# A hybrid attention, SSD and RG-LRU block on one core: first loads in two pieces, matmuls on zeros ahead of them, one more projection chunk ahead of the step sizes, and projection banks that stay open into the chunked scan

## The chip, the core and the metric

The kernel runs on one NeuronCore of a Trainium2 chip. The metric is the device time of one execution in microseconds (us), as the median of several runs. The engines are named as the profile names them: PE (TensorE's matmuls), PEld (its weight loads), DVE (VectorE), ACT (ScalarE), POOL (GpSimd) and SP (the queue that starts the DMAs).

## What is computed

One layer on 1024 tokens of width 1024. The input is normalised and multiplied with `w_in`; the columns of the product go to dilated attention, to a state space mixer (SSD) with its step sizes `dt`, and to a gated recurrence (LRU). The three results go through `w_out`, then a gated feed-forward layer and a last norm follow.

```python
h = rmsnorm(x, norm_mix)
q, k, v, z, xbc, dt_raw, g_lru, x_lru = split_cols(h @ w_in)
att = dilated_attention(q, k, v)
ssd = ssd_mixer(z, xbc, dt_raw, ssd_conv_w, ssd_conv_b, ssd_dt_bias, ssd_a_log, ssd_d, ssd_norm)
lru = rglru_mixer(g_lru, x_lru, lru_conv_w, lru_conv_b, lru_wa, lru_ba, lru_wx, lru_bx, lru_lambda)
x = x + concatenate([att, ssd, lru]) @ w_out
x = x + swiglu(rmsnorm(x, norm_ffn), w_gate, w_up, w_down)
return rmsnorm(x, norm_final)

# in ssd_mixer: a convolution and silu over xbc, the step sizes, and a scan in chunks of 128 tokens
xbc = silu(causal_depthwise_conv(xbc, conv_w, conv_b))
dt = softplus(dt_raw + dt_bias)
acs = cumsum(dt * a, axis=2)          # inside each chunk
```

## The kernel before

**Tiling.** Everything lies with channels on the 128 partitions and the 1024 tokens along a row. A float32 operand is held as a high and a low part (`hi`, `lo`, written by `split` and `wload`: the high part is an ACT copy, the low part a DVE subtraction), and each product is three matmuls: high by high, high by low, low by high. One projection chunk is 128 output columns of `w_in`: two halves of 512 tokens, each 8 x 3 matmuls of 128 x 512, 48 in all. Each half has a PSUM bank of its own, taken in turn from three (`bank`, the pool `psl`, tile name `mm`), and DVE empties it with a multiply by the norm (`e<-mm,rB`).

**First stage (lines 180 to 241).** For each of the 8 row blocks of x, `xt` is loaded, DVE or ACT writes the high part of `h` (`hi`), DVE the low part, ACT the squares. As they come, `early` puts the products of two chunks (28 and 24) into banks, and those of a third (29) afterwards. The load of x's block 0 and that of the first weights are one DMA of 512 KB each.

**The LRU and SSD chunks (lines 287 to 404).** Four LRU chunks follow; each ends in the two gate products of line 333, whose banks (pool `ps2`, two tiles `p2`) ACT reads with a sigmoid (`ri<-p`). The eight chunks that the SSD needs are called by `xbc`: `in_proj`, then `conv` (an ACT pass and three DVE passes, in the profile `bct<-e,pr` or `xs<-e,pr` at lines 78 and 268), then a silu on ACT, which needs its function table loaded. Two of the eight (`NXB = 2`) are called beside the last LRU chunk; six (`for c in XB`) after the step sizes.

**The step sizes (lines 353 to 397).** A bank pair `pd` from `ps2` takes 32 small matmuls (lines 360 to 364). ACT copies 8 rows of it (`e<-p 8x1024`), DVE adds 8 others and multiplies with the norm (`e<-p,e 8x1024` and `e<-e,rB 8x1024`), and PE transposes the result (line 370). Softplus on DVE and two more small products (lines 382, 386, 394) lead to `acs`. A DMA writes it out (`acd`), and DMAs read it back to all partitions (`acb`).

**The chunked scan (lines 407 to 577).** `pctx.close()` ends the pools of the projections. A new pool of three banks (`psm`, line 446) and the scan's own pools are opened. The scan's small steps are interleaved with units of `qkv_fill` (line 409), large products for attention (matmuls of line 423). The first unit needs the high and low parts of two weight tiles, w_in[8] and w_in[9].

**What sets the order.** The code is in program order; a scheduler then places the instructions of each engine in one fixed list, from their dependencies and its own estimates of time. Each engine takes its list in order, so an instruction that waits holds back all behind it.

Of the kernel before, what the change touches and what calls it, by code (L numbers as in the profile page):

```python
# [7 lines left out]
F32 = mybir.dt.float32  # L8
# [30 lines left out]
def tile_hybrid_block(ctx: ExitStack, tc: tile.TileContext, xT, w_in, w_dt, w_out, w_gu, w_dn, lru_g, prm,  # L39
# [8 lines left out]
    wp = ctx.enter_context(tc.tile_pool(name="wp", bufs=2))  # L48
    sm = ctx.enter_context(tc.tile_pool(name="sm", bufs=2))
    dr = ctx.enter_context(tc.tile_pool(name="dr", bufs=1, space=DRAM))  # L50
    pctx = ExitStack()
    psm = pctx.enter_context(tc.tile_pool(name="psl", bufs=3, space=PSUM))
    ps2 = pctx.enter_context(tc.tile_pool(name="ps2", bufs=2, space=PSUM))
    ps1 = pctx.enter_context(tc.tile_pool(name="ps1", bufs=1, space=PSUM))

# [9 lines left out]
    def f(ap):  # L65
        return ap.bitcast(F32)
# [10 lines left out]
    def act(out, in_, func, **kw):  # L77
        return A.activation(out=out, in_=in_, func=func, **kw)  # L78
# [5 lines left out]
    def wload(src, pool=None, le=None):  # L84
        st = wp.tile([P, S], F32, name="wst", tag="wst", bufs=2)
        dma(out=st, in_=src)
        hi = (pool or wp).tile([P, S], F32R, name="whi", tag="whi", bufs=2)
        lo = (pool or wp).tile([P, S], F32R, name="wlo", tag="wlo", bufs=2)
        split(st, hi, lo, le or V)
        return hi, lo  # L90
# [89 lines left out]
    with tc.tile_pool(name="np", bufs=2) as npool:  # L180
        sqs = []
        wdt = const.tile([P, KD, 40], F32R, name="wdt")
        V.memset(f(wdt), 0.0)
        wd = npool.tile([P, 64], F32, name="wd", tag="wd", bufs=1)
        p2t = [ps2.tile([P, S], F32, name="p2", tag="p2") for _ in range(2)]
        outs = [[t[:, :H2], t[:, H2:]] for t in p2t]
        outs.insert(1, [bank() for _ in range(2)])
        w01 = []

        def early(kk, which):  # L190
            ws = slice(kk * P, kk * P + P)
            for j in which:
                (whi, wlo), os = w01[j], outs[j]
                for n, (w, a) in enumerate(((whi, hhi[kk]), (whi, hlo[kk]), (wlo, hhi[kk]))):
                    for hf in range(2):
                        last_mm[0] = T.matmul(os[hf], lhsT=w[:, ws], rhs=a[:, hf * H2:hf * H2 + H2],  # L196
                                              start=(kk == 0 and n == 0), stop=(kk == KD - 1 and n == 2))

        last_mm = [None]
        for k in range(KD):  # L200
            xt = slot(npool, "xt", bufs=4)
            dma(out=xt, in_=xT[k * P:k * P + P, :])
            if k == 0:
                w01.append(wload(w_in[28]))
            if k == 1:
                w01.append(wload(w_in[24]))
                dma(out=ident, in_=c_ident)
                V.tensor_copy(identr, ident)
            if k == 4:
                w01.append(wload(w_in[29], pool=npool))  # L210
            hi, lo = slot(hp, "h", F32R), slot(hp, "h", F32R)
            if k % 2:
                act(hi, xt, AF.Copy, scale=pc("g_mix", k))
            else:
                V.tensor_scalar(out=hi, in0=xt, scalar1=pc("g_mix", k), scalar2=None, op0=ALU.mult)
            V.scalar_tensor_tensor(out=lo, in0=xt, scalar=pc("g_mix", k), in1=f(hi), op0=ALU.mult, op1=ALU.subtract)
            hhi.append(hi)
            hlo.append(lo)
            sqs.append(slot(npool, "sq", bufs=8))
            last_act = act(sqs[k], xt, AF.Square)  # L220
            for kk in ([0, 1] if k == 1 else range(k, k + 1) if 0 < k < KD - 1 else ()):
                early(kk, (0, 1))
        for k in range(1, KD):
            add(V, sqs[0], sqs[0], sqs[k])
        dma(out=wd, in_=w_dt)
        wdv = wd.rearrange("p (k c) -> p k c", c=8)
        act(wdt[:, :, 0:8], wdv, AF.Copy)
        sub(V, wdt[:, :, 32:40], wdv, f(wdt[:, :, 0:8]))
        rn = rnorm_small(sqs[:1], 1024.0, 1e-6, ps1)
        V.tensor_copy(rtok, rn)  # L230
        early(KD - 1, (0, 1))
        for hf in range(2):
            pb = spread(ps1.tile([P, H2], F32, name="p1", tag="p1"), rn[:, 4 * hf:4 * hf + 4])
            V.tensor_copy(rB[:, hf * H2:hf * H2 + H2], pb)
        for k in range(KD):
            early(k, (2,))
        xp0, g0, xp1 = ev(), ev(), ev()
        for dst, o in zip((xp0, g0, xp1), outs):
            for hf in range(2):
                sl = slice(hf * H2, hf * H2 + H2)  # L240
                mul(V, dst[:, sl], o[hf], rB[:, sl])
# [110 lines left out]

    dma(out=tri, in_=c_tri)
    dma(out=elast, in_=c_last)
    dtr = ev()[0:8, :]
    pd = ps2.tile([P, S], F32, name="p2", tag="p2")
    for hf in range(2):
# [85 lines left out]
            next(gen, None)  # L443

    pctx = ExitStack()
    psm = pctx.enter_context(tc.tile_pool(name="psm", bufs=3, space=PSUM))
    fill = qkv_fill()
    dsk = pc("dskip", 0, 4)
    wctx = ExitStack()
# [134 lines left out]
    next(fill)  # L584
    ssd_ctx.close()
    pctx.close()
    mm_ctx = ExitStack()
    psm = mm_ctx.enter_context(tc.tile_pool(name="psa_mm", bufs=2, space=PSUM))

# [643 lines left out]
```

## Time and profile before

| what | us |
|---|---|
| median of 3 runs (1411.64 to 1413.68) | 1412.61 |
| profiled execution, its own time | 1410.98 |
| its span, first to last instruction | 1409.2 |
| PE busy in the span | 1347.0 (96%) |
| DVE busy | 977.2 (69%) |
| ACT busy | 667.3 (47%) |
| POOL busy | 395.5 (28%) |

PE is busy for 96% of the span, so what a change can give is in the waits of PE, and in stretches where TensorE's clock is at its lower level. The profile lists who waited for whom, the instructions in order of time, the chain of work that ended last, and the granted clock of any stretch.

### The profile page before, as it was taken

Reading aid. Unit: us, or ns where it says so; the run is one execution under the profiler, and the core shown is the slowest. Engines: PE = TensorE matmul, PEld = TensorE weight load, DVE = VectorE, ACT = ScalarE, POOL = GpSimd, SP = SyncE. Lnnn points to the kernel's source line nnn. Section 1 sums busy time; section 2 is a strip of 40 time slices with the busy share of each in tenths; the row PEclk is TensorE's granted clock in tenths of the full one; section 3 lists DMA queues with packets and bytes.
Section 4 is the critical chain, followed back from the end, with each engine's and each line's share of the span. In section 5 each row is a group of like instructions: output and inputs, shape, how many; then the busy total and the mean of one; then the engine's idle time right before and its main releaser. Section 6 shows DMA issues by size and latency. Waiting matters only on the chain.

```text
span 1409.2 us, 18442 instructions
## 1 busy us (share of the span) xinstructions
PE 1347.0 (96%) x6786; PEld 1126.4 (80%) x6786; DVE 977.2 (69%) x1520; ACT 667.3 (47%) x1086; POOL 395.5 (28%) x283
## 2 busy tenths in 40 slices
PE   7999898999999999998988999999999998999996
PEld 6887688878888788887866788888877787888896
DVE  7667748988344877877696876676786765655745
ACT  5385636554233666666564433333333244543533
POOL 0022103765000000000036366665555651010103
PEclk9999999999999999999999999999999999999997
DMA  5112132342228964420364433444544357855523
GB/s 202 53 45 75 46 76 69 95 125 87 63 103 270 293 184 106 120 76 28 122 218 170 153 117 120 156 157 157 172 172 157 124 184 282 286 192 195 191 77 120
DMA packets 90266, 198.66 MB, mean 141 GB/s; under 512 B 9272, under 2 KB 23992, under 8 KB 90176
## 3 DMA queue, kind: packets, MB, share of 16 engines
q1 hardware_dynamic: 90176, 197.49, 43.1%
q8 instruction: 53, 0.87, 0.2%
q14 instruction: 37, 0.30, 0.1%
HBM read 142.64 MB, written 54.82 MB: 140 GB/s over the span
## 4 chain that ended last, share of the span: by engine, by line
PE 56%; DVE 13%; POOL 11%; DMA 8%; issue 6%; ACT 5%; SPq 0%; DVEq 0%; POOLq 0%; ACTq 0%
PE mm L98 19%; PE mm L1039 10%; PE x L911 5%; POOL t L69 5%; PE mm L911 4%; PE x L1039 3%; DMA whi<-w_gu 3%; DVE h L69 3%; PE mm L423 2%; PE pt L725 2%; PE p L196 2%; DVE wlo L69 1%; POOL t L75 1%; PE sc L681 1%; PE sc L682 1%
## 5 line engine op out<-in xcount | busy, mean ns | idle before, releaser
L98 PE MATMUL mm<-h,whi 128*128 128x512 f32 x1184 | 374.2, 395 | 1.7 <-DVE att L75 0.9
L98 PEld LDWEIGHTS mm<-h,whi 128*128 128x128 f32 x1184 | 221.2, 189 | 46.2 <-DVE e L72 1.2
L98 PE MATMUL mm<-h,wlo 128*128 128x512 f32 x592 | 232.3, 393 | 0.0
L911 PE MATMUL x<-A,h 128*128 128x512 f32 x660 | 170.0, 397 | 3.3 <-DVE h L69 2.8
L75 POOL TENSOR_TENSOR t<-whi 128x512 f32<-128x512 f32 x22 | 36.0, 1637 | 475.5 <-DMA x1d<-e 369.1
L911 PE MATMUL mm<-A,h 128*128 128x512 f32 x594 | 154.6, 400 | 2.1 <-ACT h L78 2.1
L1039 PE MATMUL mm<-h 128*128 128x512 f32 (+1 forms) x666 | 152.3, 381 | 0.0
L911 PEld LDWEIGHTS x<-A,h 128*128 128x128 f32 x660 | 123.7, 189 | 35.5 <-DVE h L69 5.2
L1039 PEld LDWEIGHTS mm<-h 128*128 128x128 f32 x666 | 122.1, 192 | 23.2
L911 PEld LDWEIGHTS mm<-A,h 128*128 128x128 f32 x594 | 112.9, 191 | 28.7 <-ACT h L78 2.5
L98 PEld LDWEIGHTS mm<-h,wlo 128*128 128x128 f32 x592 | 111.8, 189 | 23.5 <-DVE wlo L69 0.3
L911 PE MATMUL x<-h 128*128 128x512 f32 x396 | 106.5, 395 | 0.0
L69 DVE TENSOR_TENSOR h<-t,h 128x512 fp32r<-128x512 f32 x97 | 96.8, 1016 | 10.5 <-ACT h L78 10.5
L78 ACT ACTIVATE e<-x 128x512 f32<-128x512 f32 x60 | 35.7, 595 | 121.1 <-PE x L911 111.7
L69 DVE TENSOR_TENSOR h<-wst,h 128x512 fp32r<-128x512 f32 (+1 forms) x69 | 75.0, 1108 | 25.3 <-ACT h L78 23.7
L911 PEld LDWEIGHTS x<-h 128*128 128x128 f32 x396 | 75.1, 190 | 17.3
L78 ACT ACTIVATE whi<-wst 128x1024 fp32r<-128x1024 f32 x44 | 46.4, 1055 | 64.9 <-PE mm L98 52.3
L75 DVE TENSOR_TENSOR e<-mm,e 128x512 f32<-128x512 f32 x45 | 30.8, 684 | 61.3 <-POOL e L69 51.1
L69 DVE TENSOR_TENSOR wlo<-wst,whi 128x1024 fp32r<-128x1024 f32 x44 | 57.1, 1298 | 16.5 <-ACT whi L78 16.4
L69 DVE TENSOR_TENSOR h<-whi,h 128x1024 fp32r<-128x1024 f32 (+1 forms) x47 | 50.7, 1078 | 24.2 <-ACT h L78 24.1
L78 ACT ACTIVATE h<-wst 128x512 fp32r<-128x512 f32 (+1 forms) x69 | 51.9, 781 | 31.5 <-DMA whi<-sd 11.6
L1039 PE MATMUL x<-h 128*128 128x512 f32 (+1 forms) x270 | 60.8, 361 | 3.3 <-ACT h L78 3.3
(277 smaller groups left out, 2657.6 us busy)
## 6 DMA issues: line engine op xcount, KB each, us to landing
wst<-w_in SPq DMA_DIRECT2D x32, 512.0 KB, 3.7
qkl<-qkd SPq DMA_DIRECT2D x48, 256.0 KB, 5.7
wst<-w_gu SPq DMA_DIRECT2D x22, 512.0 KB, 4.3
whi<-w_gu SPq DMA_DIRECT2D x22, 512.0 KB, 5.6
wdd<-t SPq DMA_DIRECT2D x22, 512.0 KB, 4.8
sd<-wlo SPq DMA_DIRECT2D x22, 512.0 KB, 5.1
qkd<-e SPq DMA_DIRECT2D x16, 512.0 KB, 3.5
wst<-sd SPq DMA_DIRECT2D x27, 256.0 KB, 3.7
```

The costliest lines, as they stand in the source:

```text
L69: eng.tensor_tensor(out=out, in0=a, in1=b, op=ALU.subtract)
L75: return eng.tensor_tensor(out=out, in0=a, in1=b, op=ALU.add)
L78: return A.activation(out=out, in_=in_, func=func, **kw)
L98: T.matmul(ps, lhsT=w[:, ws], rhs=a[:, sl], start=(k == 0 and n == 0), stop=(k == nk - 1 and n == 2))
L196: last_mm[0] = T.matmul(os[hf], lhsT=w[:, ws], rhs=a[:, hf * H2:hf * H2 + H2], start=(kk == 0 and n == 0), stop=(kk == KD - 1 and n == 2))
L423: T.matmul(o, lhsT=a[k][:, ts], rhs=w, start=(k == 0 and n == 0), stop=(k == KD - 1 and n == 2))
L681: T.matmul(sc[:, :w], lhsT=qs[:, qc], rhs=ks[:, kc], start=True, stop=False)
L682: gate[0] = T.matmul(sc[:, :w], lhsT=qs[:, qc], rhs=kl[:, kc], start=False, stop=True)
L725: T.transpose(pt[:, j, qi * P:qi * P + P], pes[qi][:, kb * P:kb * P + P], ident)
L911: last_mm[0] = T.matmul(ps, lhsT=w[:, wi, ws], rhs=ops[k][i][:, ai], start=(start and k == 0 and n == 0), stop=(stop and k == 3 and n == 2 ...
L1039: mm = T.matmul(banks[n][:, cols], lhsT=w[:, 0, ws], rhs=a[:, 1, cols], start=(start and j == 0 and m == 0), stop=(stop and j == NP - 1 an ...
```

## The change

Four things change, and all outputs are computed as before.

1. The load of x's block 0 and that of the first weight tile are cut in two: half of x, 256 columns of weights, the other half of x, the other 768 columns. The splits of the weights, and DVE's two passes over x, follow piece by piece. Chunk 28's products of block 0 are written ahead of block 1.
2. Ten matmuls of 128 x 320 on a tile of zeros (`wdt` before it is filled) are written ahead of the first products, into a bank that the third early chunk later overwrites.
3. One more `xbc` chunk (the third of eight) is written ahead of the step sizes.
4. The pool `psl` is no longer closed ahead of the scan. The scan's `qkv_fill` keeps taking the same three banks.

```diff
-    pctx = ExitStack()
-    psm = pctx.enter_context(tc.tile_pool(name="psl", bufs=3, space=PSUM))
+    mm_ctx, pctx = ExitStack(), ExitStack()
+    psm = mm_ctx.enter_context(tc.tile_pool(name="psl", bufs=3, space=PSUM))
...
+        wu = wdt.rearrange("p k c -> p (k c)")
+        for _ in range(10):
+            T.matmul(outs[2][0][:, 0:320], lhsT=wu[:, 0:P], rhs=wu, start=True, stop=True)
...
-            dma(out=xt, in_=xT[k * P:k * P + P, :])
             if k == 0:
-                w01.append(wload(w_in[28]))
+                st = wp.tile([P, S], F32, name="wst", tag="wst", bufs=2)
+                whi, wlo = (wp.tile([P, S], F32R, name=n, tag=n, bufs=2) for n in ("whi", "wlo"))
+                w01.append((whi, wlo))
+                for sl in (slice(0, 256), slice(256, S)):
+                    ts = slice(0, H2) if sl.start == 0 else slice(H2, S)
+                    dma(out=xt[:, ts], in_=xT[0:P, ts])
+                    dma(out=st[:, sl], in_=w_in[28][:, sl])
+                    split(st[:, sl], whi[:, sl], wlo[:, sl])
+            else:
+                dma(out=xt, in_=xT[k * P:k * P + P, :])
...
-            for kk in ([0, 1] if k == 1 else range(k, k + 1) if 0 < k < KD - 1 else ()):
-                early(kk, (0, 1))
+            if k == 1:
+                early(0, (1,))
+            if k < KD - 1:
+                early(k, (0,) if k == 0 else (0, 1))
...
     dma(out=tri, in_=c_tri)
     dma(out=elast, in_=c_last)
+    xbc(XB.pop(0))
     dtr = ev()[0:8, :]
...
     pctx = ExitStack()
-    psm = pctx.enter_context(tc.tile_pool(name="psm", bufs=3, space=PSUM))
     fill = qkv_fill()
...
     pctx.close()
+    mm_ctx.close()
     mm_ctx = ExitStack()
```

The two DVE passes over x's block 0 (lines 215 and 216) run once per half in the changed code; the diff of those lines is left out here.

What this makes of the engines' lists is seen best around the step sizes. On PE, 21 of the third SSD chunk's 48 matmuls already stood ahead of the step sizes' 32; now all 48 do, and 37 of the next chunk stand between the step sizes and the transposes, as before. On ACT this stood between the end of the last LRU chunk and the step sizes (`la` is that chunk's gate, `e<-p 8x1024` the copy of the step sizes, `bct<-e,pr` the convolution of the third SSD chunk, the second `bct<-bct` its silu):

```order
L78 ACT_TABLE_LOAD
L78 ACTIVATE bct<-bct 128x1024
L78 ACT_TABLE_LOAD
L78 ACTIVATE la_1021<-la_1021 128x1024
L78 ACTIVATE e<-p_1037 8x1024
L78 ACTIVATE whi<-wst 128x1024
L78 ACTIVATE bct<-e,pr 128x1024
L78 ACTIVATE sp_1084<-dt 128x64
```

and now stands, on ACT at the same place:

```order
L78 ACT_TABLE_LOAD
L78 ACTIVATE bct<-bct 128x1024
L78 ACT_TABLE_LOAD
L78 ACTIVATE la_1037<-la_1037 128x1024
L78 ACTIVATE whi<-wst 128x1024
L78 ACTIVATE bct<-e,pr 128x1024
L78 ACT_TABLE_LOAD
L78 ACTIVATE bct<-bct 128x1024
L78 ACTIVATE e<-p_1117 8x1024
```

The copy of the step sizes has moved behind the third SSD chunk's weights, convolution, table load and silu. On DVE this stood from the last LRU chunk's scan (line 345) to the step sizes' two passes over 8 x 1024:

```order
L72 TENSOR_TENSOR ri<-la_1021,ri 128x1024
L345 SCALAR_TENSOR_TENSOR la_1021<-la,ri 128x1024
L72 TENSOR_TENSOR e<-mm,rB 128x512
L75 TENSOR_TENSOR e<-p_1037,e 8x1024
L72 TENSOR_TENSOR e<-e,rB 8x1024
```

and now stands, on DVE at the same place (the scan's line is 360 in the changed file, the convolution's 283):

```order
L72 TENSOR_TENSOR ri<-la_1037,ri 128x1024
L360 SCALAR_TENSOR_TENSOR la_1037<-la,ri 128x1024
L72 TENSOR_TENSOR e<-mm,rB 128x512
L69 TENSOR_TENSOR wlo<-wst,whi 128x1024
L283 SCALAR_TENSOR_TENSOR bct<-e,pr,bct 128x1021
L283 SCALAR_TENSOR_TENSOR bct<-e,pr,bct 128x1022
L283 SCALAR_TENSOR_TENSOR bct<-e,pr,bct 128x1023
L75 TENSOR_TENSOR e<-p_1117,e 8x1024
L72 TENSOR_TENSOR e<-e,rB 8x1024
```

The same chunk's low weights and three convolution passes have come in between. Behind the step sizes the lists of PE hold 77 projection matmuls up to the product of line 382 (87 before), and 103 from the last transposes of line 394 to the scan (122 before); from there on the lists are nearly the same.

## Rows read from the trace of the kernel before

**Rows 1.** Waits of PE up to 260 us: who waited, total us, times, longest.

```profile
PE p L196 <- ACT whi L78: 7.7, 1, 7.7
PE p L360 <- ACT ri L78: 5.6, 1, 5.6
```

**Rows 2.** Timeline of the first stage: start, length, engine, line, operation.

```profile
9.53 1.28 DVE L216 SCALAR_TENSOR_TENSOR h<-xt,pr,h 128x1024 fp32r<-128x1024 f32 x1 [0.59 <-ACT h L78]
...
10.46 1.91 PE L196 MATMUL p<-h,whi 128*128 128x512 f32 x4
...
12.17 1.05 PE L196 MATMUL p<-h,wlo 128*128 128x512 f32 x2
...
12.66 1.22 DVE L69 TENSOR_TENSOR wlo<-wst,whi 128x1024 fp32r<-128x1024 f32 x1
...
14.67 0.63 PE L196 MATMUL mm<-h,wlo 128*128 128x512 f32 x2
```

**Rows 3.** The chain that ended last, 130 to 235 us: start, length, what.

```profile
145.05 0.65 PE p L360
...
154.94 8.41 PE mm L98 x37
163.35 0.59 PE p L370 x8
...
189.06 0.89 PE p L394 x8
...
193.40 13.32 DMA acb<-acd
```

**Rows 4.** Busy times by stretch; before the last two numbers the granted clock and DMA.

```profile
143.30:150.10 6.80, 5.05 (x12) 1.85 (x13) 3.16 (x3) 6.73 (x7) 2.68 (x1) 0.50 0.26 80
...
221.80:225.20 3.40, 2.90 (x13) 2.93 (x14) 3.40 (x12) 3.38 (x5) 1.27 (x2) 0.50 0.00 0
```

**Rows 5.** Timeline of PE ahead of the step sizes and at the scan.

```profile
139.03 0.39 PE L98 MATMUL mm<-h,wlo 128*128 128x512 f32 x1
...
222.30 0.76 PE L423 MATMUL mm<-whi,h 128*128 128x256 f32 x2 [3.00 <-DVE e L72]
```

**Rows 6.** Timeline of ACT around the step sizes.

```profile
138.14 1.28 ACT L78 ACT_TABLE_LOAD   x1 [5.61 <-DVE bct L268]
139.44 1.06 ACT L78 ACTIVATE bct<-bct 128x1024 f32<-128x1024 f32 x1
...
154.28 1.06 ACT L78 ACTIVATE la<-la 128x1024 f32<-128x1024 f32 x1
155.37 1.02 ACT L78 ACTIVATE e<-p 8x1024 f32<-8x1024 f32 x1
```

**Rows 7.** Timeline of DVE around the step sizes and at the scan.

```profile
131.17 3.06 DVE L69 TENSOR_TENSOR wlo<-wst,whi 128x1024 fp32r<-128x1024 f32 x1
134.16 3.90 DVE L268 SCALAR_TENSOR_TENSOR bct<-e,pr,bct 128x1021 f32<-128x1021 f32 x3
...
156.71 2.29 DVE L345 TENSOR_TENSOR_SCAN la<-la,ri 128x1024 f32<-128x1024 f32 x1
158.91 0.67 DVE L72 TENSOR_TENSOR e<-mm,rB 128x512 f32<-128x512 f32 x1
159.50 1.20 DVE L75 TENSOR_TENSOR e<-p,e 8x1024 f32<-8x1024 f32 x1
160.73 1.87 DVE L72 TENSOR_TENSOR e<-e,rB 8x1024 f32<-8x1024 f32 x1
...
163.13 1.20 DVE L69 TENSOR_TENSOR wlo<-wst,whi 128x1024 fp32r<-128x1024 f32 x1
...
224.74 1.21 DVE L69 TENSOR_TENSOR wlo<-wst,whi 128x1024 fp32r<-128x1024 f32 x1
```

**Rows 8.** Timeline of POOL: its multiplies in the last two LRU chunks.

```profile
130.75 2.40 POOL L72 TENSOR_TENSOR g<-la,g 128x1024 f32<-128x1024 f32 x1 [9.17 <-DVE la L345]
...
159.13 2.40 POOL L72 TENSOR_TENSOR g<-la,g 128x1024 f32<-128x1024 f32 x1 [10.37 <-issue]
```

More of the change, by code (lines that the diff above doesn't have):

```diff
@@ L211, in tile_hybrid_block @@
             hi, lo = slot(hp, "h", F32R), slot(hp, "h", F32R)
[L212 to L216, printed above, removed]
+            for ts in ((slice(0, H2), slice(H2, S)) if k == 0 else (slice(0, S),)):
+                if k % 2:
+                    act(hi, xt, AF.Copy, scale=pc("g_mix", k))
+                else:
+                    V.tensor_scalar(out=hi[:, ts], in0=xt[:, ts], scalar1=pc("g_mix", k), scalar2=None, op0=ALU.mult)
+                V.scalar_tensor_tensor(out=lo[:, ts], in0=xt[:, ts], scalar=pc("g_mix", k), in1=f(hi[:, ts]),
+                                       op0=ALU.mult, op1=ALU.subtract)
             hhi.append(hi)
```

## The prediction

> **What bounds the kernel now.** I read the busy shares first: PE is busy for 96% of the span, so the waits of PE are what can be won. Up to the scan they are few. PE starts at 7.7 us, when the first weights have been split, and waits 5.6 us ahead of the step sizes for a gate's bank [rows 1]; the scan's first unit waits 3.00 us for DVE to empty a bank [rows 5]. Next I read the pace. The first matmuls of 128 x 512 come (12.17 - 10.46) / 4 = 0.43 us apart [rows 2], later ones 8.41 / 37 = 0.227 [rows 3], so TensorE begins at the lower of its two levels (1.2 instead of 2.4 GHz). It falls back to it after the two waits: the granted clock is 0.50 in 143.3 to 150.1 us and in 221.8 to 225.2 [rows 4]. All three places are aimed at. Last I read the chain that ended last. From the step sizes to the scan it does not stay on PE: it leaves the last transposes, passes the DMA `acb` of 13.3 us and returns to PE at the scan [rows 3]. So ACT, DVE and a DMA are near the bound there too, and what PE wins it keeps only where they keep pace.
>
> **Start.** The first pieces of x and of the weights let PE begin some 2.5 us sooner. But block 1 of x is not loaded earlier: the bytes ahead of it are the same. Its low part ends on DVE at 9.53 + 1.28 = 10.81 [rows 2]. Chunk 28's 6 matmuls of block 0 are then done; of block 1's 6 matmuls, 4 follow that low part, so at the lower level they end near 10.81 + 4 x 0.43 = 12.5, where before they ended at 12.17 + 2 x 0.43 = 13.0: 0.5 us won. At the full level they would end sooner, but PE then needs the low weights of chunk 24, which DVE ends at 12.66 + 1.22 = 13.88; before, those matmuls began at 14.67 [rows 2]. So at most 0.8 us is won however early PE starts. Two more DMAs ahead of block 1 and three more DVE instructions can cost some 0.3. I take a gain of 0.4 (0.8 to a loss of 0.3). The ten matmuls on zeros lie where PE was idle, cost nothing, and can only move the clock.
>
> The Trainium skill ("TensorE: Matmul & The Clock Gate", Part 1, on what is actually happening) says that the throttled clock is the default and that activity releases it; by that the zeros make the first 12 matmuls run at full pace, 12 x 0.2 = 2.4 us, and the sum below would be 2.0 lower. The rows of the feed speak against it.
>
> **The chunk ahead of the step sizes: PE.** The last projection matmul before the wait starts at 139.03 [rows 5], so PE is free at 139.26. The 27 matmuls that are moved in fill 27 x 0.227 = 6.13 us, to 145.39. The bank is free at 145.05 [rows 3]: the wait is gone. The 32 small matmuls now run at full pace, about 32 x 0.23 = 7.36, to 152.75, and the 37 behind them take 8.41, to 161.16. There the transposes of line 370 could start; before, they started about 163.3 [rows 3].
>
> **The chunk ahead of the step sizes: ACT and DVE.** The transposes need the step sizes, and the order of ACT and DVE has put the third SSD chunk ahead of them, as the lists in the section on the change show. From the rows of before: DVE's scan of the last LRU chunk ends at 156.71 + 2.29 = 159.0, the emptying of a bank at 159.6 [rows 7]. Then come the low weights. POOL multiplies from 159.13 to 161.53 [rows 8]. When the same DVE instruction met POOL's multiply of 130.75 to 133.15, it took 3.06 us and ended 1.08 after it, against 1.20 alone [rows 7, 8]; so it ends near 162.6. The convolution takes 3.90 [rows 7], to 166.5. ACT's table load waits for it (the row of 138.14 does the same, 0.08 us after a convolution's end), 1.28 long, and the silu takes 1.06 behind it [rows 6], to 168.95; the copy of the step sizes takes 1.02, to 170.0, where before it ended at 156.4 [rows 6]. DVE adds (1.20, to 171.2) and multiplies. That row is 1.87 long, but POOL was at work then and is not now, so I take 1.2 [rows 7, 8]: 172.4. PE would wait from 161.2 to 172.4, 11.2 us, twice what was removed.
>
> Compared by progress: the transposes start 172.4 - 163.3 = 9.1 us later, with 6.13 us more of PE's work done before them: 3.0 lost. The lower bound has low weights that POOL does not hold (1.9 less): 1.1 lost. The upper has the multiply at 1.87: 3.7 lost. All instructions of this chain hang on the last LRU chunks' gates and so on PE; they move with the gain at the start.
>
> **The clock after that wait.** The 163.3 of before already holds the slow restart of the step sizes: 12 matmuls at 0.43 instead of 0.23, 2.4 us. A wait of 11 us brings the lower level at least as surely, and the projection matmuls behind the transposes pay it: again 2.4, at least 1.4 (half of the 2.9 busy us in the second stretch of rows 4), at most 3.4 (half of a 6.8 us stretch). So this edit costs 3.0 + 2.4 = 5.4 us (1.1 + 1.4 = 2.5 to 3.7 + 3.4 = 7.1).
>
> The Trainium skill ("ScalarE: Activation LUTs", What ACT_TABLE_LOAD costs) counts a drain of about 1.38 us to each load. The row does not show it: load at 138.14, 1.28 long, next instruction at 139.44 [rows 6]. With it the sum would be 1.4 higher.
>
> **The banks kept into the scan.** If the wait of 3.00 and the slow restart after it (1.4) went, 4.4 would be won. What is late next: the unit needs the second weight's low part, and DVE ends that at 224.74 + 1.21 = 225.95 [rows 7], 36.0 us after the last transposes (189.06 + 0.89 = 189.95 [rows 3]). In the changed lists one convolution no longer stands behind `acb`, so that DVE work comes about 3.9 us sooner after the transposes, at 32.1. PE has 122 - 103 = 19 matmuls fewer in between, 4.3 us. The two nearly cancel: PE starts the unit early, does 12 matmuls, then waits for DVE. I take nothing, from a gain of 1.0 to a loss of 1.2. The chunk order costs no DMA: SP's list past the start is the same.
>
> **The sum.** -0.4 + 5.4 + 0 = +5.0 us. The profiled execution of 1410.98 would become 1416.0. The median of the runs stands 1.6 above it, and I add the 5.0 to the median: 1412.6 + 5.0 = **1417.6 us**. Its bounds: 2.5 - 0.8 - 1.0 = +0.7 (1413.3) to 7.1 + 0.3 + 1.2 = +8.6 (1421.2). Past the scan the lists are nearly the same and PE's waits there hang on chains that shift as a whole, so nothing gives the loss back.
>
> **Rivals.**
>
> *The waits simply go* (faster). The start wins 0.8, the step sizes 5.6 + 2.4, the scan 4.4: 13.2 us, 1399.4. It speaks for it that the profile names these waits singly. It decides at the transposes: the step sizes would have to be ready by 161.2, and the rows give 172.4. A shift of 11 us in lists that each engine takes in order is not to be seen. 6%; another 3% lie between this and the next.
>
> *Near enough to nothing* (same). The chain at its lower bound, +2.5, and the kept banks worth about half of their 4.4, with the start at -0.4: about 0, 1412.6. It decides at the scan: DVE would have to bring the second low weights some 2 us sooner than the 32.1 above. For it: the wait's row names only the bank. 19%.
>
> *The wait moves on once more* (slower). The product of line 382 waits for softplus on DVE. That chain starts 9.1 us later, and PE has 77 instead of 87 matmuls (2.3 us less) ahead of it. With the slow restart PE just stays behind it by my count; if DVE needs 3 us more, mixed with two more convolutions, PE waits there too: 1420.6. 12%.
>
> **How the numbers follow.** The forecast, with its bounds, has 60%, the rivals 6 + 3, 19 and 12. About 0.2% (2.8 us) is what a measurement of this kernel tells from no change. Faster by more: 6 and 2 of the 3, 0.08. Within: 19, the third of the 3, and 3 from the forecast's low end, 0.23. Slower by more: 57 + 12, 0.69. The range leaves out the first rival and the farthest ends: 1411.5 to 1421.0.
>
> **What would show it.** In the changed profile the wait of line 360's successor is gone, and PE waits some 11 us ahead of the transposes of 8 x 1024 (line 386 there), with a granted clock of 0.5 behind it; ACT's copy `e<-p 8x1024` follows the silu of `bct` and a table load. The scan's first unit starts without a wait and stops after 12 matmuls for DVE. PE meets chunk 24's low weights at most 0.8 us sooner than at 14.67. I am wrong if PE passes the transposes with a wait under 6 us, or if the first stage wins over 1 us.

## The result: 0.8% slower, 11.4 us

Measured side by side on one chip, the kernel before took 1413.14 us (median of 4 runs, 1411.64 to 1414.73) and the changed kernel 1424.81 (4 runs, 1423.98 to 1426.88). The ratio is 1.0081, with a 95% interval of 1.0068 to 1.0094: 11.4 us lost (9.6 to 13.3). The direction and the main place were forecast, the size was not: 5.0 us were forecast, 8.4 at most.

The profiled execution of the changed kernel took 1426.88 us. Of its page, the span and the busy times (engine, us, share, instructions):

```profile
span 1425.1 us, 18469 instructions
PE 1357.5 (95%) x6796; PEld 1135.5 (80%) x6796; DVE 979.6 (69%) x1523; ACT 666.5 (47%) x1086; POOL 392.6 (28%) x283
```

PE is busy 10.5 us longer (1347.0 before). The ten small matmuls on zeros are 3.0 of them; the rest is the same list of matmuls done at a lower clock. Next, the waits of PE up to 260 us in the changed kernel (who waited for whom, total us, times, longest), against [rows 1]:

```profile
PE p L386 <- DVE e L72: 11.4, 1, 11.4
PE mm L439 <- DVE e L72: 2.2, 1, 2.2
PE p L199 <- ACT h L78: 1.9, 1, 1.9
...
PE mm L439 <- DVE wlo L69: 1.3, 1, 1.3
PE p L199 <- DVE h L227: 0.7, 1, 0.7
```

The wait of 5.6 us ahead of the step sizes is gone, and one of 11.4 stands ahead of the transposes of line 386. The timeline of ACT, DVE and PE there (start, length, engine, line, operation, in brackets the wait just before it):

```profile
157.37 1.04 ACT L78 ACTIVATE whi<-wst 128x1024 fp32r<-128x1024 f32 x1
161.62 3.11 DVE L69 TENSOR_TENSOR wlo<-wst,whi 128x1024 fp32r<-128x1024 f32 x1
164.65 3.91 DVE L283 SCALAR_TENSOR_TENSOR bct<-e,pr,bct 128x1021 f32<-128x1021 f32 x3
168.64 1.28 ACT L78 ACT_TABLE_LOAD   x1 [5.66 <-DVE bct L283]
169.93 1.06 ACT L78 ACTIVATE bct<-bct 128x1024 f32<-128x1024 f32 x1
171.01 1.01 ACT L78 ACTIVATE e<-p 8x1024 f32<-8x1024 f32 x1
172.06 1.21 DVE L75 TENSOR_TENSOR e<-p,e 8x1024 f32<-8x1024 f32 x1 [3.50 <-ACT e L78]
173.31 1.21 DVE L72 TENSOR_TENSOR e<-e,rB 8x1024 f32<-8x1024 f32 x1
174.57 1.01 PE L386 MATMUL p<-ident,e 8*128 8x8 f32 x8 [11.42 <-DVE e L72]
```

This is the predicted chain link by link: low weights at 3.1 us, convolution, table load, silu, copy, add, multiply. The granted clock behind the wait, and at the scan's first unit (busy us of PE, PEld, DVE, ACT, POOL; then the granted clock, the DMA share, GB/s):

```profile
174.50:180.00 5.50, 5.42 (x19) 4.50 (x20) 2.28 (x9) 1.79 (x3) 0.00 (x0) 0.52 0.00 0
...
231.00:237.80 6.80, 5.52 (x25) 5.22 (x26) 6.80 (x11) 5.43 (x10) 3.36 (x3) 0.50 0.17 50
```

Both stretches are at the lower level of 1.2 GHz, which answers [rows 4].

To say where the time went, I use two places that every kernel passes once. Place A is the first gate product of the third LRU chunk, ahead of the step sizes. Place B is the first set of sixteen 128x1 products of line 138 behind the scan. Their rows, of the kernel before:

```profile
107.19 0.39 PE L333 MATMUL p<-xh,ghi 128*128 128x512 f32 x1
...
394.31 1.84 PE L138 MATMUL p<-ones,e 128*128 128x1 f32 x16
```

and of the changed kernel:

```profile
108.91 0.39 PE L348 MATMUL p<-xh,ghi 128*128 128x512 f32 x1
...
402.16 1.84 PE L138 MATMUL p<-ones,e 128*128 128x1 f32 x16
```

A second trace of the kernel before (e8) has 106.55 and 393.47. Against the mean of the two traces (106.87 and 393.89) the changed kernel is 2.0 us behind at A and 8.3 at B. A second trace of the changed kernel (e10) is 8.4 behind at B. All kernels:

| kernel | us behind at A | us behind at B | us lost at the end (95% interval) |
|---|---|---|---|
| the change; again (e10) | 2.0; 2.8 | 8.3; 8.4 | 11.4 (9.6 to 13.3); 11.9 (9.5 to 14.3) |
| e1 split alone | 3.4 | 4.0 | 3.1 (1.7 to 4.4) |
| e2 zeros alone | 0.0 | 1.1 | 1.6 (0.1 to 3.0) |
| e3 chunk alone | -0.1 | 5.5 | 7.1 (5.2 to 8.9) |
| e4 banks alone | -0.2 | -1.4 | 0.0 (-1.4 to 1.4) |
| e5 steps first | -0.4 | -2.3 | -1.8 (-3.5 to 0.0) |
| e6 cut by partitions | 1.4 | 1.1 | 4.0 (1.8 to 6.1) |
| e7 split and zeros | 2.3 | 1.7 | 4.4 (2.3 to 6.4) |
| e8 before again | -0.3 | -0.4 | -0.7 (-3.0 to 1.6) |
| e9 change, loads whole | 0.3 | 6.4 | 9.0 (6.9 to 11.3) |
| e11 banks, exponentials later | 0.3 | -3.8 | -2.8 (-4.5 to -1.0) |
| e12 steps first, exponentials later | -0.9 | -10.3 | -9.2 (-11.4 to -7.1) |
| e13 two tiny loads | 0.5 | 1.1 | 1.0 (-0.8 to 2.7) |
| e14 weights cut only | 2.0 | 1.3 | 2.7 (0.7 to 4.8) |
| e15 e12 with cut loads, zeros | 1.0 | -7.5 | -5.5 (-7.6 to -3.4) |

The last column is the ratio to the runs of before on the same chip, in us. One of the six executions of e15 took 2152 us at a mean granted clock of 0.57 and does not count in its number. A and B are read from one trace of each kernel. Kernels with the old start lie between -0.9 and 0.5 at A, so a difference under 0.9 there says nothing; and e2, which does the same work between A and B as the kernel before, is 1.1 behind at B, so a difference of about 1 there says little.

A third place lies between the two: the first product of the scan, ahead of which every kernel has done the same matmuls. Its rows in the kernel before, in the changed kernel and in e3, the moved chunk alone:

```profile
218.53 0.38 PE L465 MATMUL pA<-ident,xs 128*128 128x128 f32 x2
```

```profile
224.93 0.38 PE L480 MATMUL pA<-ident,xs 128*128 128x128 f32 x2
```

```profile
222.20 0.38 PE L466 MATMUL pA<-ident,xs 128*128 128x128 f32 x2
```

The kernel before has 218.14 in its second trace (e8), so 218.34 in the mean.

### The profile page after: what moved, and what is told of

Its sections match the earlier page's. It is cut to its first block, busy times and chain, and to the rows that moved or that the text cites. A ratio compares the mean times of both kernels' runs of the same rounds, so it can differ in the third digit from the quotient of the medians.

```text
span 1425.1 us, 18469 instructions
## 1 busy us (share of the span) xinstructions
PE 1357.5 (95%) x6796; PEld 1135.5 (80%) x6796; DVE 979.6 (69%) x1523; ACT 666.5 (47%) x1086; POOL 392.6 (28%) x283
## 4 chain that ended last, share of the span: by engine, by line
PE 57%; DVE 10%; DMA 7%; POOL 7%; issue 4%; ACT 2%; SPq 1%; DVEq 0%; POOLq 0%; ACTq 0%
PE mm L98 15%; PE x L927 10%; PE mm L1055 10%; PE mm L927 8%; PE x L1055 3%; POOL t L69 3%; DMA whi<-w_gu 2%; PE pt L741 2%; PE mm L439 2%; DVE h L69 2%; PE sc L697 1%; PE sc L698 1%; PE po L755 1%; PE po L757 1%; DVE wlo L69 1%
## 5 line engine op out<-in xcount | busy, mean ns | idle before, releaser
L98 PE MATMUL mm<-h,whi 128*128 128x512 f32 x1184 | 378.2, 399 | 0.9 <-DVE att L75 0.9
L98 PEld LDWEIGHTS mm<-h,whi 128*128 128x128 f32 x1184 | 224.3, 192 | 46.2 <-DVE att L75 1.1
L927 PEld LDWEIGHTS x<-h 128*128 128x128 f32 x396 | 75.3, 190 | 17.2
L78 ACT ACTIVATE whi<-wst 128x1024 fp32r<-128x1024 f32 (+2 forms) x45 | 46.6, 1035 | 66.9 <-PE mm L98 50.9
L69 DVE TENSOR_TENSOR wlo<-wst,whi 128x1024 fp32r<-128x1024 f32 (+2 forms) x45 | 59.2, 1315 | 24.6 <-ACT whi L78 24.4
```

The lines of the kernel that those rows point to most:

```text
L69: eng.tensor_tensor(out=out, in0=a, in1=b, op=ALU.subtract)
L98: T.matmul(ps, lhsT=w[:, ws], rhs=a[:, sl], start=(k == 0 and n == 0), stop=(k == nk - 1 and n == 2))
L927: last_mm[0] = T.matmul(ps, lhsT=w[:, wi, ws], rhs=ops[k][i][:, ai], start=(start and k == 0 and n == 0), stop=(stop and k == 3 and n == 2 ...
```

## The experiments

### The four parts, each alone

**e1**, the start's split alone:

```diff
+                for sl in (slice(0, 256), slice(256, S)):
+                    ts = slice(0, H2) if sl.start == 0 else slice(H2, S)
+                    dma(out=xt[:, ts], in_=xT[0:P, ts])
+                    dma(out=st[:, sl], in_=w_in[28][:, sl])
+                    split(st[:, sl], whi[:, sl], wlo[:, sl])
```

> The kernel before with one edit: the first loads of x and of the weights in two pieces, with their splits, and chunk 28's products of block 0 ahead of block 1. No matmuls on zeros, no moved chunk, old banks. My theory now: this edit alone loses 1.6 us (1.2 to 2.0), because the small pieces take longer to land in all and x's block 1 lands later: DVE's low part of block 1 starts at about 10.8 us instead of 9.53 [rows 2], PE starts near 5.0 instead of 7.73 but then waits, and everything up to 139 us lies 1.3 to 1.7 us later. Rival 1 (the prediction's step): 0.4 us won. Rival 2 (the later loss comes from here too, by shifted lists far behind): more than 3 us lost.

Measured: 3.4 us behind at A, 4.0 at B, 3.1 lost at the end. The prediction's step, a gain of 0.4, is out; the loss is also larger than the 1.6 that I read from the trace of the whole change. It has the size of rival 2, but not its place: all of it is there at A already.

**e2**, the zeros alone:

```diff
+        for _ in range(10):
+            T.matmul(outs[2][0][:, 0:320], lhsT=wu[:, 0:P], rhs=wu, start=True, stop=True)
```

> The kernel before with one edit: ten matmuls of 128 x 320 on zeros ahead of the first products. My theory: nothing, within 0.4 us of the kernel before; the first products still come 0.43 us apart. Rival 1 (the zeros bring the full clock forward): the first 12 products at 0.23 us, up to 2.4 us won. Rival 2 (they make PE late or keep the full clock back): 0.5 us or more lost.

Measured: A as before, and the first twelve products 0.43 us apart as before. The end is 1.6 us later, with an interval that nearly reaches zero. The lists of all other engines are the same row for row, so what lies between A and the end here is not explained by work that moved. At the scan the profile shows what differs. PE waits 3.03 us there, as in both traces of the kernel before, and then e2 runs at the lower clock to 228 us (granted clock ahead of the last two numbers):

```profile
222.00:225.00 3.00, 2.69 (x12) 2.72 (x13) 3.00 (x12) 2.98 (x5) 1.06 (x2) 0.50 0.00 0
225.00:228.00 3.00, 3.00 (x16) 3.00 (x16) 3.00 (x3) 2.73 (x6) 1.62 (x2) 0.50 0.25 67
```

and e8, the kernel before, keeps the upper one after the same wait:

```profile
222.00:225.00 3.00, 3.00 (x25) 3.00 (x26) 3.00 (x10) 2.98 (x4) 1.41 (x2) 1.00 0.00 0
```

The first trace of before lies in between: it was slow from 221.8 to 225.2 [rows 4]. So the slow restart at the scan comes and goes by execution.

**e3**, the chunk alone:

```diff
     dma(out=elast, in_=c_last)
+    xbc(XB.pop(0))
     dtr = ev()[0:8, :]
```

> The kernel before with one edit: one more SSD chunk written ahead of the step sizes. My theory: PE waits about 11 us ahead of the transposes of 8 x 1024 and runs at the lower clock behind them; 5.5 us lost (4.5 to 7) at the end, and about that at 205 us already. Rival 1 (the whole loss of the change is this edit's, its delay grows behind the scan): 9 to 11 us lost. Rival 2 (the wait costs little by itself, the loss needs the kept banks too): under 3 us.

Measured: 5.5 us behind at B, 7.1 lost at the end. PE waits 11.2 us ahead of the transposes. This edit carries most of the loss, by the predicted mechanism. But the 5.5 are not there at once, as I expected: at the scan's first product e3 is 3.9 behind (222.20), and 1.6 more come by B, where PE's wait for a bank has grown from 3.00 us [rows 5] to 4.48:

```profile
227.46 0.48 PE L424 MATMUL mm<-whi,h 128*128 128x256 f32 x2 [4.48 <-DVE e L72]
```

**e4**, the banks alone:

```diff
-    psm = pctx.enter_context(tc.tile_pool(name="psl", bufs=3, space=PSUM))
+    psm = mm_ctx.enter_context(tc.tile_pool(name="psl", bufs=3, space=PSUM))
...
-    psm = pctx.enter_context(tc.tile_pool(name="psm", bufs=3, space=PSUM))
```

> The kernel before with one edit: the three projection banks stay open into the scan. My theory: PE starts the scan's first unit about 3 us sooner, does 12 matmuls and waits for the second weight's low part; the end moves by less than 1.0 us either way. Rival 1 (the wait of 3.00 us and the slow restart simply go): 3 to 4.4 us won. Rival 2 (the bank that is shared by projections and scan comes free later, several units further on): 2 to 4 us lost.

Measured: 1.4 us ahead at B, nothing at the end. PE waits 0.84 us for the bank and 1.92 for the low weights (one wait of 3.00 before, [rows 5]): the wait changed its name.

The ends of e7 (split and zeros together, below), e3 and e4 add up to 4.4 + 7.1 + 0.0 = 11.5, against the 11.4 of the change. That the parts do not work on each other is not shown by it: each end is known to some 2 us, and at B the same three add up to 1.7 + 5.5 - 1.4 = 5.8, against 8.3.

### Why the start loses

**e7**, split and zeros together (the diffs of e1 and e2):

> The kernel before with two edits: the first loads in pieces, and the ten matmuls on zeros. My theory: the zeros give the split back a part: progress at 100 us is 1.7 us behind the kernel before (1.2 to 2.2), as in the changed kernel, against 3.1 with the split alone; 1 to 3 us lost at the end. Rival 1 (the two simply add): 3 us or more behind at 100 us, and 4 to 5 us lost at the end. Rival 2: no loss at 100 us.

Measured: 2.3 behind at A, less than the split alone, as expected; 4.4 lost at the end, more than expected. Its timeline of PE shows what the zeros do:

```profile
7.82 0.63 PE L199 MATMUL p<-h,wlo 128*128 128x512 f32 x2
11.35 2.54 PE L199 MATMUL p<-h,whi 128*128 128x512 f32 x4 [2.90 <-ACT h L78]
...
16.05 0.62 PE L199 MATMUL p<-h,whi 128*128 128x512 f32 x2
```

At 7.82 us two matmuls take 0.63 us together, the upper level. Then PE waits 2.9 us for x's block 1, and the next ones take 0.43 each again, until about 16. In the changed kernel the zeros did not show even that; its timeline of PE:

```profile
10.86 2.54 PE L199 MATMUL p<-h,whi 128*128 128x512 f32 x4 [1.90 <-ACT h L78]
13.19 1.06 PE L199 MATMUL p<-h,wlo 128*128 128x512 f32 x2
14.05 1.91 PE L199 MATMUL mm<-h,whi 128*128 128x512 f32 x4
15.75 0.70 PE L199 MATMUL p<-h,whi 128*128 128x512 f32 x2
16.29 0.63 PE L199 MATMUL mm<-h,wlo 128*128 128x512 f32 x2
```

The Trainium skill ("TensorE: Matmul & The Clock Gate", Part 1, What's actually happening) has throttled as the default, which activity releases; e7's 0.63 at 7.82 agrees, and its 2.54 behind the wait shows the way back.

So the cut start pays twice. Block 1 lands later, and PE, which began early and then stood, comes to its full pace near 15.8 us. In the kernel before, the four matmuls from 13.02 us come 0.30 apart and those from 14.21 0.23, so the change falls near 13.6:

```profile
13.02 1.36 PE L196 MATMUL mm<-h,whi 128*128 128x512 f32 x4
...
14.21 0.62 PE L196 MATMUL p<-h,whi 128*128 128x512 f32 x2
```

The traces' own records of the clock agree: the upper level is first recorded at 13.6 us in the kernel before and at 12.1 in e8, at 15.9 in the changed kernel and at 17.2 in e10. In all ten traces with whole first loads, zeros or not, it lies between 10.3 (e12) and 13.6 us; in the six with loads cut by columns between 14.3 (e15) and 18.1 (e1), if in e7 the second rise is taken, at 15.8. (Up to that first record the clock column of the profile reads 1.00, though the pace of 0.43 shows the lower level.)

SP also starts the load of block 1 later, behind two more transfers. In the kernel before

```profile
2.13 0.43 SPq L202 DMA_DIRECT2D xt<-xT  x1
```

and in the changed kernel, with DVE's pass for the low part of block 1 (at 9.53 in [rows 2]):

```profile
3.07 0.43 SPq L215 DMA_DIRECT2D xt<-xT  x1
...
10.84 1.28 DVE L228 SCALAR_TENSOR_TENSOR h<-xt,pr,h 128x1024 fp32r<-128x1024 f32 x1 [0.66 <-ACT h L78]
```

**e6**, the same number of pieces with rows of 4 KB:

```diff
+                for rs in (slice(0, 64), slice(64, P)):
+                    dma(out=xt[rs, :], in_=xT[rs, :])
+                    dma(out=st[rs, :], in_=w_in[28][rs, :])
+                split(st, whi, wlo)
```

> The kernel before with its first two loads cut into two pieces each by partitions (64 rows of 4 KB) and not by columns; the splits still wait for the whole. As many DMAs as in the changed kernel, with the same bytes. Theory 1 (short rows make the pieces slow): x's block 1 lands as before, near 8.3 us (8.0 to 8.7), and PE's progress at 100 us is within 0.5 us of the kernel before. Theory 2 (two more DMAs to start and to finish are what costs): block 1 lands at 9.2 us or later, progress 1 us or more behind.

Measured: block 1's pass on ACT starts at 9.89 us (8.35 before), 1.4 behind at A. That contradicts the theory of short rows, but does not prove the other: SP starts block 1's load 1.56 us later here (at 3.69), and these pieces were slow themselves. Between 2 and 8 us (last two numbers: share of the DMA engines, GB/s) the kernel before had

```profile
2.00:8.00 6.00, 0.27 (x1) 0.27 (x2) 2.33 (x3) 2.33 (x4) 0.00 (x0) 1.00 0.96 337
```

the changed kernel

```profile
2.00:8.00 6.00, 4.76 (x15) 3.48 (x14) 2.81 (x5) 1.69 (x4) 0.00 (x0) 1.00 0.91 297
```

and e6

```profile
2.00:8.00 6.00, 0.00 (x0) 0.00 (x0) 0.46 (x1) 0.72 (x3) 0.00 (x0) 1.00 0.96 205
```

In all three the DMA engines are busy nearly all the time; they move less. e6 shows one thing more: its PE starts 2 us later than before, but does not stop, and is at full pace by 13.51 (two matmuls in 0.62 us), earlier than the changed kernel that started at 4.96.

The Trainium skill ("DMA: Bandwidth & Descriptors", Specifications) gives 512 bytes as the least for full rate. By that the pieces, of rows from 1 to 4 KB, would move at the full rate; the 297 and 205 GB/s beside 337 disagree.

**e13**, the number of transfers alone:

```diff
+            if k == 1:
+                dma(out=tiny[0:1, :], in_=w_in[28][0:1, 0:128])
+                dma(out=tiny[1:2, :], in_=w_in[28][1:2, 0:128])
             dma(out=xt, in_=xT[k * P:k * P + P, :])
```

> The kernel before with two more loads of 512 bytes each ahead of x's block 1; the order of all other work is the same. Theory 1 (it is the rate at which the pieces are moved): block 1's pass on ACT starts within 0.5 us of the kernel before (8.35), and the first gate product of line 333 near 107 us is within 0.6 us. Theory 2 (it is the number of transfers that the queue has to start): block 1's pass starts 0.9 us or more later, near 9.3, and the gate product 1 us or more later.

Measured: block 1's pass on ACT starts at 9.04 us, 0.7 later, between the two theories; A is 0.5 behind, within the spread. Nine traces with the old loads have this pass between 7.63 and 8.87 us, so the 0.7 stands just outside their spread; what is sure is that SP starts the load later, at 2.78 instead of 2.13 us. PE, which still begins at its old time, hardly loses by it. Between 2 and 8 us e13 moves 310 GB/s at a share of 0.89. So two more transfers lower the rate too, by engines that stand, while the cut loads lower it with the engines busy: divided by the share, 348 here and 351 before, 326 in the changed kernel.

**e14**, only the weights cut:

```diff
+                for sl in (slice(0, 256), slice(256, S)):
+                    dma(out=st[:, sl], in_=w_in[28][:, sl])
+                    split(st[:, sl], whi[:, sl], wlo[:, sl])
```

> The kernel before with only the first weights cut by columns (256 and 768); x's block 0 is one load. My theory: rows of 1 KB and 3 KB cost little, so block 1's pass on ACT starts 0.3 to 0.7 us later than 8.35, under half of the 1.3 us of the changed kernel, and the gate product near 107 us lies under 1 us behind. Rival (any cut costs the whole): 1.2 us or more later.

Measured: block 1's pass starts at 9.14, about as in e13, but A is 2.0 behind and not 0.5. My expectation missed. The difference between e13 and e14 is that PE starts at 6.85 us here, stops 0.6 us for block 1, and still takes 0.43 a matmul until 16.1. At A, the early start that can't go on is worse than the later one that can. At B the two kernels are level (1.3 and 1.1), and their ends overlap.

### Whether the order of ACT and DVE is what costs

**e5** has the banks kept and the moved chunk's matmuls ahead of the step sizes, but its convolution and silu behind them (the same way the low weights of the chunk after next):

```diff
+    in_proj(16 + c3, xp3)
     dtr = ev()[0:8, :]
...
+    dmul = mul(V, dtr, dtr, rB[0:8, :])
+    with tc.issue_after(dcp.ins), tc.issue_after(dmul.ins):
+        conv(y3, xp3, "scw", "scb", c3)
+        act(y3, y3, AF.Silu)
...
+        if n == 1:
+            with tc.issue_after(dmul.ins):
+                w = wload(w_in[16 + c])
```

> Kept banks and the moved chunk without the split loads and the zeros, and with one thing more: only the moved chunk's matmuls go ahead of the step sizes; its convolution and silu, and the low weights of the chunk after next, are held behind the step sizes' copy and two DVE passes. My theory (it is the order of ACT and DVE that costs, not the moved matmuls): PE waits at most 1.5 us ahead of the transposes, the clock stays up there, and PE is 6 to 8 us ahead of the kernel before at that point; the scan's start then hangs on the step sizes' chain and the read-back, which begin some 3 us sooner, so 2 to 5 us are won at the end. Rival 1 (the later chain takes everything back): within 1 us of the kernel before. Rival 2 (PE's gain is kept whole): 7 to 9 us won. Rival 3 (the moved matmuls themselves cost): 3 us or more lost.

Measured: the wait ahead of the transposes is 1.6 us, and 1.8 us are won at the end (2.3 at B). The clock is up over the wait but not behind it, against my theory:

```profile
163.00:166.40 3.40, 3.40 (x10) 2.69 (x9) 3.40 (x5) 0.00 (x0) 0.00 (x0) 0.54 0.33 72
```

So the moved matmuls do not cost; what went ahead of the step sizes on ACT and DVE does. PE passes the transposes 1.3 us sooner (161.97 against 163.28) with 26 more matmuls done (5.9 us), and is still 6.5 us ahead at the scan's first product (211.82 against 218.34). It gives most of that back in the scan's first unit. ACT's timeline shows where:

```profile
197.78 1.28 ACT L78 ACT_TABLE_LOAD   x1
209.64 1.70 ACT L78 ACTIVATE yx<-acb 64x256 f32<-64x256 f32 x4 [10.57 <-DMA acb<-acd]
211.36 1.06 ACT L78 ACTIVATE whi<-wst 128x1024 fp32r<-128x1024 f32 x1
```

ACT stands 10.57 us for the read-back, and behind the waiting exponentials in its list are the weights and the convolution that the scan's first unit needs. The kernel before has the same wait, 10.03 us at 206.74.

**e11** takes that out of the kernel before with kept banks:

```diff
+                with tc.issue_after(conv_last[0].ins):
-                act(yx[es, 1], pB[es].rearrange("p (a e) i -> p a e i", e=2)[:, :, e, :], AF.Exp)
+                    act(yx[es, 1], pB[es].rearrange("p (a e) i -> p a e i", e=2)[:, :, e, :], AF.Exp)
```

> The kernel before with kept banks, and with ACT's four exponentials of acb held behind the last SSD chunk's first convolution pass on ACT, so that ACT does not stand waiting for the read-back with weights and convolutions behind it. My theory (kept banks win nothing because ACT waits 10 us for acb, and DVE and the second weight with it): the waits of 3 us at the scan's start shrink to under 1 us and the slow restart goes, 3 to 5 us won at 250 us and at the end. Rival (DVE's own work is the bound there, whenever ACT starts): under 1.5 us won.

Measured: PE's waits at the scan's start fall to one of 0.6 us, no stretch at the lower clock is left there, 3.8 us won at B and 2.8 at the end, a little under the range. This is what the fourth part of the change was after; kept banks alone (e4) gave 1.4 at B and nothing at the end. The exponentials held back without the kept banks were not tried, so what each of the two is worth there is not separated.

**e12** is e5 with that edit:

> The kernel of e5 (kept banks, the moved chunk's matmuls ahead of the step sizes, its convolution behind them) and ACT's exponentials of acb held back as in e11. My theory: it keeps most of what PE gains at the step sizes: 6 to 8 us ahead of the kernel before at 250 us, and 5 to 8 us won at the end. Rival 1 (another chain, the read-back of acb for the second chunk's products, takes it back): 2 to 4 us won, as e5. Rival 2: no better than e11 alone.

Measured: 10.3 us ahead at B, 9.2 won at the end (ratio 0.9935, 0.9919 to 0.9950; median 1403.77 us), more than I expected. It beats both kernels. Against e5 nearly all of it comes in the scan's first unit: at the scan's first product e12 is 7.3 us ahead of the kernel before, e5 6.5. The clock stays up behind the wait at the transposes here, which was as long in e5. PE's wait ahead of the transposes, and the exponentials on ACT, in its timeline:

```profile
161.47 0.66 PE L380 MATMUL p<-ident,e 8*128 8x8 f32 x8 [1.59 <-DVE e L72]
...
214.83 1.70 ACT L78 ACTIVATE yx<-acb 64x256 f32<-64x256 f32 x4
```

**e15** puts the cut loads and the zeros on e12:

> The kernel of e12 with the changed kernel's start as well: loads in pieces, and zeros. My theory: the start's loss is kept to the end in this kernel too: 2 to 3 us slower than e12, so 5.5 to 7.5 us won on the kernel before. Rival (the start's loss is made good later, where PE waits for others): within 1 us of e12's 0.9935, 8.5 to 9.5 us won.

Measured: 1.9 behind e12 at A, 2.8 at B, and 3.7 at the end (-5.5 against -9.2). The start's loss is kept.

### Behind the scan

**e8** is the kernel before, and **e10** the changed kernel, each unchanged; **e9** is the changed kernel with its loads whole (the diff of e1 left out).

> The kernel before, unchanged, for a second trace. My theory: behind the scan its trace shows drops of the clock that the first trace of it does not have, near 420, 675 and 1200 us, and ends 2 to 4 us later than the first at the same lists: the profiled run of before was one of its quick ones. Rival: the same drops at the same places as the first trace, to 0.5 us; then the drops of the changed kernel are its own.

> The changed kernel with one part undone: the first loads whole again (zeros, moved chunk and kept banks stay). Its lists behind the scan are those of the kernel before, row for row. My theory: progress at 417 us, ahead of the attention, is 5.2 us behind the kernel before (4.5 to 6.0), some 2 us better than the changed kernel there, and the end follows: 5 to 7 us behind before. Rival 1 (the tail of the changed kernel is slow because its lists there differ a little): the same at 417, and at the end 4 us or more better than the changed kernel. Rival 2 (the combination of moved chunk and kept banks costs more than the parts): 7.5 us or more behind at 417.

> The changed kernel, unchanged, for a second trace and more times. My theory: 7.5 to 8.5 us behind the first trace of before at 417 us once more, to 0.6 us, since that part repeats; from there to the end it loses a different amount than the first trace's 8.2 us, between 3 and 8, because the drops of the clock behind the scan come and go by execution. Rival: again 8 us lost from 417 to the end; then its tail is slower by itself.

Measured: e8 ends 4.1 us later than the first trace of the same kernel (2 to 4 expected) and loses 4.9 from B on. Stretches of lower clock near 463 and 671 us are longer and one near 1200 is new, which is two of the three places that I named; in all, the traces' records of the clock have 49.5 us at the lower level behind B against 43.9, worth 2.8 us. So the profiled run of before, 1410.98, was a quick one; 15.9 us between the two profiled runs overstate the loss. e10 repeats B to 0.2 us and then loses 6.7 against the first trace of before, within my range. e9 is 6.4 behind at B, 1.9 better than the change and a little over its range, and 9.0 at the end, over its range too: the rows behind the scan are those of before, and yet it loses 2.6 more there, so different lists are not the cause. In all, 3.1 us of the 11.4 arise behind B (1.3 to 5.0 by the interval of the end). The feed-forward layer seems to show a part; PE's waits there, before:

```profile
PE x L911 <- DVE h L69: 1.2, 2, 0.7
```

and in the changed kernel:

```profile
PE x L927 <- DVE h L69: 4.0, 4, 1.5
```

e10 has 3.1, e8 1.8. But these waits do not carry the 3.1. All waits of PE behind B add up to 32.4 us before and 35.2 in e8, and to 35.9 and 33.4 in the two traces of the change. And the waits shown are as long in e15 (3.5), which is faster than before, and short in e3 (1.3), which is slower. The time at the lower level behind B is 57.5 us in the change, 58.5 in e10 and 57.5 in e9; but e4 and e11, whose ends are no later than that of the kernel before, have 56.2. Where the 3.1 come from stays open.

## Why the prediction was wrong, step by step

- **What bounds the kernel.** Right. All three places that it named moved the time, and ACT, DVE and the read-back did take over from PE at the scan, as e5 and e11 show.
- **Start: the step that failed.** Predicted -0.4 (0.8 won to 0.3 lost), measured 2.0 and 2.8 lost at A in the two traces of the change. The step was to take block 1's arrival as unmoved: DVE's pass for its low part, fixed at 9.53 from [rows 2], began at 10.84. "The bytes ahead of it are the same" was true, but SP starts the load at 3.07 in place of 2.13, and the bytes move at 297 GB/s in place of 337 between 2 and 8 us. The 0.3 for two more DMAs and three more DVE instructions was too small: e13 shows 0.7 of delay beside two more transfers alone. And the count of PE's time took the lower level as ending where it did; in the changed kernel, where PE starts early and stops twice, it lasts some 2.2 us longer (15.8 against 13.6), which is 1.1 us of work. The ceiling of 0.8 on the gain was sound. In e9, with whole loads and zeros, the upper level is recorded at 10.6 us already, and PE then waits for the low weights of chunk 24, as forecast:

```profile
14.46 0.73 PE L199 MATMUL mm<-h,wlo 128*128 128x512 f32 x2 [0.40 <-DVE wlo L69]
```

  That is 0.2 sooner than the 14.67 of [rows 2], and nothing is won at A (0.3 behind). What the forecast lacked was a floor.
- **The zeros.** "Cost nothing, and can only move the clock": right at A (e2, 0.0; e9, 0.3). That they bring the upper level forward is not shown: e2 has it at 13.2 us and e9 at 10.6, within the 10.3 to 13.6 of the kernels without them. In e7 it came early, at 5.6 us, and was lost over the wait for block 1.

  The Trainium skill ("TensorE: Matmul & The Clock Gate", Part 1, What's actually happening) has activity release the clock, and by that the prediction would have had 2.4 us more; no run here gained them.
- **The chunk, PE and ACT and DVE.** Right: a wait of 11.2 us forecast, 11.4 measured; transposes at 172.4 forecast, 174.57 measured, of which 1.7 is the late start. The low weights held by POOL took 3.11 (3.06 in [rows 7]), the multiply 1.21 (1.2 taken). The table load, which the prediction counted without a drain, ends at 169.92, and the silu starts at 169.93.
- **The clock behind that wait.** Right in kind; the stretch at 0.52 from 174.5 to 180 answers the forecast. Both together: +5.4 forecast. At the scan's first product 3.9 are lost in e3, 4.4 in e9 (223.00, less 0.3 at A) and 4.6 in the change (less 2.0 at A). That is within the range of 2.5 to 7.1; that e3 has 5.5 at B is luck in part, since 1.6 of it arise at the scan, where the forecast had nothing.
- **The kept banks.** Right in the sum, half right in the path. 0 forecast; e4 gives 1.4 at B and 0.0 at the end, and on top of the chunk they change nothing: from the scan's first product to B, e9 and e3 both take 177.2 us (175.8 and 175.3 before). PE does stop after 12 matmuls, but for the emptying of a bank (2.2), and only 12 matmuls later for the second low weights (1.3), the wait that was named. Of the 4.4 us that the prediction saw in this place, the 1.4 for the slow restart were no fixed sum: e8 has the wait without it.
- **"Nothing gives the loss back", and nothing adds to it.** The first half held. The second was never weighed: 3.1 us more arise behind B, and why stays open.
- **The sum.** 5.0 became 11.4: 2.4 to 3.2 from the start, 3.1 from behind B, and under 1 from the rest. The rivals with a win were rightly small; none of them was the case.

## What to carry to other kernels

When a load is cut so that an engine can begin sooner, follow the next load too: here its transfer started later, the pieces moved more slowly, and PE, which began early and then stood, lost more than it did by beginning late and going on. When matmuls are moved ahead to fill a wait, look at what they bring along on the other engines: here the matmuls were free (e5), and the convolution and silu behind them cost the wait again, twice over (11.4 us for 5.6). Where an instruction waits for a transfer of 13 us, look at what is queued behind it on its engine: with four small exponentials held back, the kept banks won 3.8 us at B and 2.8 at the end, and without that 1.4 and nothing. And take a second trace before a stretch at the lower clock is counted as a price: the one at the scan lasted 3.4 us, 6 or more, or was not there, in executions with the same wait.

## What the runs showed of the hardware

- Cutting a load lowered the rate while the DMA engines stayed busy: 337 GB/s whole, 297 cut by columns, 205 cut into halves of 64 partitions (between 2 and 8 us).
- With two transfers of 512 bytes ahead of it, SP started the next 512 KB 0.65 us later, and its first use came 0.7 later (one trace).
- PE that started at 9.73 us without a break (e6) was at full pace by 13.51; PE that started at 4.96 with waits of 0.7 and 1.9 us (the changed kernel), only by 15.8. With whole first loads the upper level came between 10.3 and 13.6 us, with loads cut by columns between 14.3 and 18.1.
- Behind the same wait of 3.0 us at the scan, the clock stayed up (e8), or was at 0.50 for 3.4 us (the first trace of before) or from 222 to 228 us (e2).
- A table load of 1.28 us on ACT was followed by its function after 0.01 us.
- Two executions of the same kernel differ by 4.9 us from 394 us to the end, with lists that are the same.
